# The FFNs' activated tiles in four groups, read by the second matrix's products four columns from each group in turn

## The chip, the core and the metric

The kernel runs on one core of a Trainium2 chip. The metric is the device time of one execution in microseconds (us); 2208.91 us is the median of three runs before the change. The engines are named as the profile names them: PE is TensorE (the products), PEld its weight loads, DVE VectorE, ACT ScalarE, POOL GpSimd, SP SyncE.

## What is computed

One inference step of a decoder layer over 256 prompt tokens and 32 sample tokens, 288 tokens in all, with a model width of 2048: a gated FFN, a recurrent mixer, and a second gated FFN, each between two RMSNorms. The change is in the two FFNs alone:

```
D_MODEL = 2048
D_FF = 5632

def swiglu(x, w_in, w_out):
    gate, up = jnp.split(x @ w_in, 2, axis=-1)
    return (jax.nn.silu(gate) * up) @ w_out

x = x + 0.5 * rmsnorm(swiglu(rmsnorm(x, g[0]), ffn1_w_in[l], ffn1_w_out[l]), g[1])
...
x = x + 0.5 * rmsnorm(swiglu(rmsnorm(x, g[4]), ffn2_w_in[l], ffn2_w_out[l]), g[5])
```

## The kernel before

Activations stand with the channels on the 128 partitions and the 288 tokens along the free axis: one tile of 128 x 288 for each 128 channels. A product takes 128 x 128 weights as the stationary operand, streams 288 columns of activations, and adds 128 x 288 sums into a PSUM tile.

Everything is split into a high and a low part, both of type float32r, so one float32 product is three products: high weights by high activations (L596), high weights by low activations (L597), low weights by high activations (L598). The function `mm3` yields these three. The weights come by DMA on SP's queue as `raw` tiles of 128 x 1024 (512 KB); ACT copies the high part into a `wh` tile (L100), DVE subtracts to get the low part (L101). Three `raw` and four `wh` buffers are in turn, so that the splitting runs ahead of the products.

The function `block` makes one group of output columns: 512 wide, so four PSUM tiles (f = 0 to 3), over `nk` tiles of the contraction (k). A `wh` unit holds two k. For each unit the order is f, then k, then the three products, 24 products a unit. The order on every engine is the order in which the code is written, with some instructions moved behind a named one.

The FFN function `ffn` cuts the 5632 hidden channels into 11 chunks of 512. For chunk c, `do_in` makes a `gate` and an `up` block (nk = 16, from the tiles `xh`, `xl`). `ev_up` takes a finished `up` tile: DVE multiplies it by the norm's row (L691) and by the gate (L692), ACT writes the high part into `hh` (L693), DVE the low part into `hl` (L694). `do_out` then makes four `out` blocks (o = 0 to 3) from `hh` and `hl` with 4 k for each chunk and adds the result to `y` (L782). The chunks are staggered: in 0, in 1, out 0, in 2, out 1, up to in 10, and last one out stage over the chunks 9 and 10 together (nk = 8). So each FFN has 10 out stages: nine that an in stage follows, and the last one.

Before the change `hh` and `hl` are tiles of 128 x 4 x 288: for each of the chunk's four k the 288 tokens lie one behind the other, 1152 bytes. A column of the products' moving operand is one token.

Of the kernel before, what the change touches and what calls it, by code (L numbers as in the profile page):

```python
# [9 lines left out]
F32 = mybir.dt.float32  # L10
F32R = mybir.dt.float32r
U8 = mybir.dt.uint8
AF = mybir.ActivationFunctionType
# [18 lines left out]
RAW_BUFS = 3  # L32
HL_BUFS = 4
HALF = 1024 + 32
SCAN_LAG = 4
X_EARLY = 12

# [93 lines left out]
def trunk_kernel(ctx, tc, x_prompt, x_sample, state_gla, state_hgrn, norm_gains, f1_in, f1_out, f2_in, f2_out,  # L131
# [455 lines left out]
    def block(name, nk, rhs, evac, width=512, tick=None, tail=1, hold=False, most=99, fill=None, late=0, byk=(), lag=0, skip=()):  # L587

        nf, per = width // P, 1024 // width
        nu = nk // per  # L590
        ps = [mmtile(f"{name}_{f}") for f in range(nf)]
        ws = [W.next() for _ in range(EARLY // per)] if fill else []

        def mm3(dst, w, f, k, parts, start, stop):
            a, c = k % per, slice(f * P, f * P + P)
            yield lambda: PE.matmul(dst, w[0][:, a, c], parts[0], start=start, stop=False)  # L596
            yield lambda: PE.matmul(dst, w[0][:, a, c], parts[1], start=False, stop=False)  # L597
            yield lambda: PE.matmul(dst, w[1][:, a, c], parts[0], start=False, stop=stop)  # L598

        def mm(w, f, k):  # L600
            if not fill or f or k >= EARLY:
                for ready in mm3(ps[f][:, 0:T], w, f, k, rhs(k), k == 0, k == nk - 1):
                    product[0] = ready().ins

        if fill:
            fill.products(lambda dst, k, parts, stop: mm3(dst, ws[k // per], 0, k, parts, k == 0, stop), ps[0][:, 0:T])
        for u in range(nu - tail):
            w = ws.pop(0) if ws else W.next()
            if u not in byk:
                for f in range(nf):  # L610
                    for k in range(u * per, (u + 1) * per):
                        mm(w, f, k)
                    if tick is not None and f % 2:
                        tick(u * per + f // 2)
            for k in range(u * per, (u + 1) * per) if u in byk else ():
                if fill and k < UPDATED:

                    fs = range(1 if k < EARLY else 0, nf)
                    threes = [list(mm3(ps[f][:, 0:T], w, f, k, rhs(k), k == 0, False)) for f in fs]
                    for three in threes:  # L620
                        three[0]()
                        product[0] = three[2]().ins
                    with tc.issue_after(product[0]):
                        for three in threes:
                            product[0] = three[1]().ins
                elif k < late:

                    threes = [list(mm3(ps[f][:, 0:T], w, f, k, rhs(k), k == 0, False)) for f in range(nf)]
                    for ready in [r for t in threes for r in t[:2]] + [t[2] for t in threes]:
                        product[0] = ready().ins  # L630
                else:
                    for f in range(nf):
                        mm(w, f, k)
                if tick is not None:
                    tick(k)
            if u not in skip and not (lag and u == nu - tail - 1):
                W.ahead(most)
            if fill and u == 5:
                fill.scaled()
        ws = [W.next() for _ in range(tail)]  # L640
        ks = range((nu - tail) * per, nk)
        ticked = 0
        for f in range(nf):
            for k in ks:
                mm(ws[k // per - (nu - tail)], f, k)
            ins = evac(f, fill.total(ps[f][:, 0:T]) if fill and f == 0 else ps[f][:, 0:T])
            while tick is not None and (ticked + 1) * nf <= (f + 1) * len(ks):
                tick(ks[ticked])
                ticked += 1
            if lag and f == lag:  # L650
                with tc.issue_after(ins):
                    W.ahead(most)
        if not hold:
            W.ahead()
# [4 lines left out]
    def ffn(tag, gcol, gnext, pn, before, fill=None):  # L659
# [3 lines left out]
        with ExitStack() as pools:  # L663
# [1 line left out]
            hid, final_tiles = {}, []  # L665

            def do_in(c):
                hh = fp.tile([P, 4, T], F32R, name=f"hh{tag}_{c}", tag="hh")
                hl = fp.tile([P, 4, T], F32R, name=f"hl{tag}_{c}", tag="hl")
                hid[c] = (hh, hl)  # L670
                gs = []

                def gate(g):
                    def run():
                        V.tensor_tensor(g, g, rt, op=ALU.mult)
                        act(g, g, AF.Silu)
                    return run

                def ev_gate(f, ps):
                    g = fp.tile([P, T], F32, name="g", tag="g", bufs=6)  # L680
                    gs.append(g)
                    if c == 0:
                        W.behind = S.activation(g, ps, AF.Copy).ins
                        pn.late.append(gate(g))
                    else:
                        V.tensor_tensor(g, ps, rt, op=ALU.mult)
                        act(g, g, AF.Silu)

                def ev_up(f, ps):
                    u = fp.tile([P, T], F32, name="u", tag="u", bufs=3)  # L690
                    ins = V.tensor_tensor(u, ps, rt, op=ALU.mult).ins  # L691
                    V.tensor_tensor(u, u, gs[f], op=ALU.mult)  # L692
                    S.activation(hh[:, f, :], u, AF.Copy)  # L693
                    V.tensor_tensor(hl[:, f, :], u, hh[:, f, :].bitcast(F32), op=ALU.subtract)  # L694
                    return ins

                if c == 0:
                    block(f"gate{tag}_0", KT, xrhs, ev_gate, tick=pn.tick0, most=1 if final else 0, fill=fill,
                          late=0 if final else FIRST, byk=range(KT))
                    before.close()  # L700
                    if not final:
                        border.append(Border(mixer_start, hg1, gnext, 5, 2))
                else:
                    block(f"gate{tag}_{c}", KT, xrhs, ev_gate, byk=(2,) if c == 1 else ())
                if final and c == 0:
                    last_pool()
                block(f"up{tag}_{c}", KT, xrhs, ev_up, tick=pn.tick1 if c == 0 else None,
                      byk=(0,) if c == 1 or final and c == 0 else (), lag=int(c == 0))

# [49 lines left out]
            def do_out(c, n):  # L759
# [8 lines left out]
                for o in range(4):  # L768
                    def ev(f, ps):
# [17 lines left out]
                        if end:  # L787
                            if not final:
                                border[0].fill.new(k)
                            elif k < KT - 1:  # L790
# [6 lines left out]
                                else:  # L797
                                    if f > 1:
                                        by_token(zs[f - 2], k - 2, *zt)
                                    zs.append(z)  # L800
                    block(f"out{tag}_{c}_{o}", 4 * n, lambda k: [t[:, k % 4, :] for t in hs[k // 4]], ev,
                          tail=2 if end and o == 3 else 1, hold=end and o == 3)
                    k = 4 * (c - 4) + o
                    if final and 0 <= k < KT:
# [928 lines left out]
```

## Time and profile before

| | us |
|---|---|
| runs | 2209.27, 2208.91, 2207.38 |
| median | 2208.91 |
| span of the profiled execution | 2206.5 |

The profile is of one execution of its own; its span runs from the first to the last instruction, and what lies around it isn't listed apart: the runs are 0.9 to 2.8 us longer than the span.

| engine | busy us | share of the span |
|---|---|---|
| PE | 2198.2 | 100% |
| PEld | 2182.2 | 99% |
| DVE | 1385.7 | 63% |
| ACT | 1020.1 | 46% |
| POOL | 180.0 | 8% |

A busy PE does not mean a PE at its peak: a product's record includes its way through the array, so records overlap, and what counts is the distance from one start to the next. In the rows of groups, a line, an engine and an operation are followed by the tile written and the tiles read, the shape and the count; behind the bar stand the busy time in us, the mean of one in ns, the engine's idle time just before them in us and what ended it. In the view by stretches each row has the stretch in us from the span's start, its length, the busy time of each engine with the number of instructions that touch the stretch, the granted clock, the DMA engines' share and GB/s.

### The profile page before, as it was taken

Reading aid. Unit: us, or ns where it says so; the run is one execution under the profiler, and the core shown is the slowest. Engines: PE = TensorE matmul, PEld = TensorE weight load, DVE = VectorE, ACT = ScalarE, POOL = GpSimd, SP = SyncE. Lnnn points to the kernel's source line nnn. Section 1 sums busy time; section 2 is a strip of 40 time slices with the busy share of each in tenths; the row PEclk is TensorE's granted clock in tenths of the full one; section 3 lists DMA queues with packets and bytes.
Section 4 is the critical chain, followed back from the end, with each engine's and each line's share of the span. In section 5 each row is a group of like instructions: output and inputs, shape, how many; then the busy total and the mean of one; then the engine's idle time right before and its main releaser. Section 6 shows DMA issues by size and latency. Waiting matters only on the chain.

```text
span 2206.5 us, 43225 instructions
## 1 busy us (share of the span) xinstructions
PE 2198.2 (100%) x17828; PEld 2182.2 (99%) x17828; DVE 1385.7 (63%) x2253; ACT 1020.1 (46%) x1537; POOL 180.0 (8%) x327
## 2 busy tenths in 40 slices
PE   9999999999999999999999999999999999999998
PEld 9999999999999999999999999999999999999998
DVE  7545546555555568888888755844555466556646
ACT  6443433343344345655676654543333333333344
POOL 2000000000000001233210000000000020122005
PEclk9999999999999999999999999999999999999999
DMA  7655555555555554667566564555555565666555
GB/s 223 174 166 171 169 168 170 171 165 171 172 166 180 179 166 142 194 207 216 173 189 176 176 190 135 169 167 171 171 166 170 172 176 172 180 179 179 172 164 161
DMA packets 227334, 384.87 MB, mean 174 GB/s; under 512 B 21362, under 2 KB 60864, under 8 KB 227136
## 3 DMA queue, kind: packets, MB, share of 16 engines
q1 hardware_dynamic: 213872, 365.02, 55.1%
q0 software_dynamic: 10992, 16.77, 2.8%
q8 instruction: 140, 2.29, 0.4%
q10 hardware_dynamic: 2272, 0.31, 0.1%
q14 instruction: 58, 0.48, 0.1%
HBM read 363.75 MB, written 11.80 MB: 170 GB/s over the span
## 4 chain that ended last, share of the span: by engine, by line
PE 98%; DVE 1%; ACT 1%; issue 0%; POOL 0%; DVEq 0%; ACTq 0%; POOLq 0%
PE gate L597 10%; PE gate L596 10%; PE gate L598 10%; PE up L597 8%; PE out L597 8%; PE up L596 8%; PE up L598 8%; PE out L596 8%; PE out L598 8%; PE hfq L596 2%; PE hfq L597 2%; PE mo L597 2%; PE hfq L598 2%; PE mo L596 1%; PE mo L598 1%; PE hi L597 1%
## 5 line engine op out<-in xcount | busy, mean ns | idle before, releaser
L101 DVE TENSOR_TENSOR wh<-raw,wh 128x1024 fp32r<-128x1024 f32 (+1 forms) x676 | 821.7, 1217 | 610.2 <-ACT wh L100 609.1
L100 ACT ACTIVATE wh<-raw 128x1024 fp32r<-128x1024 f32 (+1 forms) x676 | 711.0, 1053 | 943.1 <-PE gate L598 295.2
L597 PE MATMUL gate<-xl,wh 128*128 128x288 f32 x1660 | 490.1, 297 | 0.0
L598 PE MATMUL gate<-xh,wh 128*128 128x288 f32 x1660 | 483.6, 293 | 0.0
L596 PE MATMUL gate<-xh,wh 128*128 128x288 f32 x1660 | 483.0, 292 | 0.0
L597 PE MATMUL out<-hl,wh 128*128 128x288 f32 x1408 | 419.2, 298 | 0.0
L597 PE MATMUL up<-xl,wh 128*128 128x288 f32 x1408 | 419.2, 298 | 0.0
L598 PE MATMUL up<-xh,wh 128*128 128x288 f32 x1408 | 411.6, 292 | 0.0
L598 PE MATMUL out<-hh,wh 128*128 128x288 f32 x1408 | 411.5, 292 | 0.0
L596 PE MATMUL out<-hh,wh 128*128 128x288 f32 x1408 | 409.3, 291 | 0.0
L596 PE MATMUL up<-xh,wh 128*128 128x288 f32 x1408 | 409.3, 291 | 0.0
L596 PEld LDWEIGHTS gate<-xh,wh 128*128 128x128 f32 x1660 | 313.7, 189 | 0.8 <-DVE u L691 0.4
L598 PEld LDWEIGHTS gate<-xh,wh 128*128 128x128 f32 x1660 | 311.4, 188 | 0.2 <-DVE wh L101 0.2
L597 PEld LDWEIGHTS gate<-xl,wh 128*128 128x128 f32 x1660 | 310.2, 188 | 0.5
L596 PEld LDWEIGHTS out<-hh,wh 128*128 128x128 f32 x1408 | 266.8, 189 | 0.2 <-DVE y L782 0.2
L596 PEld LDWEIGHTS up<-xh,wh 128*128 128x128 f32 x1408 | 266.7, 189 | 0.0
L598 PEld LDWEIGHTS up<-xh,wh 128*128 128x128 f32 x1408 | 264.5, 188 | 0.0
L598 PEld LDWEIGHTS out<-hh,wh 128*128 128x128 f32 x1408 | 264.5, 188 | 0.0
L597 PEld LDWEIGHTS up<-xl,wh 128*128 128x128 f32 x1408 | 263.8, 187 | 0.0
L597 PEld LDWEIGHTS out<-hl,wh 128*128 128x128 f32 x1408 | 263.7, 187 | 0.0
L782 DVE TENSOR_TENSOR y<-out,y 128x288 f32<-128x288 f32 x287 | 120.7, 452 | 82.1 <-PE out L598 81.1
L739 POOL DMA_DIRECT2D xT<-b x64 | 37.1, 586 | 757.3 <-PE gate L598 566.7
(417 smaller groups left out, 2559.1 us busy)
## 6 DMA issues: line engine op xcount, KB each, us to landing
raw<-in_ffn_w_in_dram SPq DMA_DIRECT2D x350, 512.0 KB, 3.6
raw<-in_ffn_w_out_dram SPq DMA_DIRECT2D x176, 512.0 KB, 3.6
raw<-in_mix_w_in_dram SPq DMA_DIRECT2D x64, 512.0 KB, 4.3
raw<-in_mix_w_in_dram SPq DMA_DIRECT2D x96, 256.0 KB, 3.2
raw<-in_mix_w_out_dram SPq DMA_DIRECT2D x32, 512.0 KB, 3.7
out_dram<-s POOLq DMA_DIRECT2D x32, 256.0 KB, 2.9
s<-in_state_gla_dram SPq DMA_DIRECT2D x16, 256.0 KB, 5.9
s<-in_state_hgrn_dram SPq DMA_DIRECT2D x16, 256.0 KB, 5.6
```

The source lines that it names most:

```text
L100: i1 = self.nc.scalar.activation(h[:, a, c], raw[:, a, c], AF.Copy).ins
L101: i2 = self.nc.vector.tensor_tensor(l[:, a, c], raw[:, a, c], h[:, a, c].bitcast(F32), op=ALU.subtract).ins
L596: yield lambda: PE.matmul(dst, w[0][:, a, c], parts[0], start=start, stop=False)
L597: yield lambda: PE.matmul(dst, w[0][:, a, c], parts[1], start=False, stop=False)
L598: yield lambda: PE.matmul(dst, w[1][:, a, c], parts[0], start=False, stop=stop)
L739: queues[n % len(queues)].dma_start(dst[q * TS:(q + 1) * TS, 4 * g:4 * g + 4, :, cols].rearrange("p k t c -> p (k t) c"), b32[rows, q])
L782: V.tensor_tensor(y[k], ps, y[k], op=ALU.add)
```

## The change

Each `hh` and `hl` tile becomes 128 x 4 x 4 x 80. The 288 tokens of one k are cut into four groups of 72, and a group has 80 places, so that the groups begin 320 bytes apart and eight places of each stay unused. A k takes 1280 bytes instead of 1152, and each of the four buffers grows by 512 bytes a partition. ACT and DVE write the groups through the same pattern (4 x 72).

The products of the out blocks read these tiles in turns: four columns from group 0, four from group 1, four from group 2, four from group 3, then the next four of each, 18 turns. The PSUM tile is addressed in the same way, its 288 columns as four groups of 72 without gaps, so each token's sum lands at the column where it landed before, and what reads the PSUM tile is unchanged. `mm3` takes this path where the activations have three dimensions, which only the FFNs' `out` blocks give it.

```diff
+LINE = 4
+PLACES = 4
+
+def columns(t):
+    return t.rearrange("p (g c) -> p g c", g=PLACES)
+
+def turns_of(t):
+    return t.rearrange("p g (i e) -> p i g e", e=LINE)
...
         def mm3(dst, w, f, k, parts, start, stop):
             a, c = k % per, slice(f * P, f * P + P)
+            if len(parts[0].shape) == 3:
+                dst, parts = turns_of(columns(dst)), [turns_of(t) for t in parts]
             yield lambda: PE.matmul(dst, w[0][:, a, c], parts[0], start=start, stop=False)
...
-                hh = fp.tile([P, 4, T], F32R, name=f"hh{tag}_{c}", tag="hh")
-                hl = fp.tile([P, 4, T], F32R, name=f"hl{tag}_{c}", tag="hl")
+                hid[c] = [fp.tile([P, 4, PLACES, 80], F32R, name=f"h{j}{tag}_{c}", tag=f"h{j}") for j in "hl"]
+                hh, hl = ([t[:, f, :, 0:T // PLACES] for f in range(4)] for t in hid[c])
                 hid[c] = (hh, hl)
...
-                    S.activation(hh[:, f, :], u, AF.Copy)
-                    V.tensor_tensor(hl[:, f, :], u, hh[:, f, :].bitcast(F32), op=ALU.subtract)
+                    S.activation(hh[f], columns(u), AF.Copy)
+                    V.tensor_tensor(hl[f], columns(u), hh[f].bitcast(F32), op=ALU.subtract)
...
-                    block(f"out{tag}_{c}_{o}", 4 * n, lambda k: [t[:, k % 4, :] for t in hs[k // 4]], ev,
+                    block(f"out{tag}_{c}_{o}", 4 * n, lambda k: [t[k % 4] for t in hs[k // 4]], ev,
```

No instruction changes its place on any engine; lines move down by 15. On PE, at the start of the first out block (`out_0_0_0` is chunk 0, o = 0, f = 0; `hh_0`, `hl_0` are chunk 0's tiles), there stands before:

```order
L596 MATMUL out_0_0_0_1463<-hh_0_235,wh_1351 128x288
L597 MATMUL out_0_0_0_1463<-hl_0_236,wh_1351 128x288
L598 MATMUL out_0_0_0_1463<-hh_0_235,wh_1351 128x288
L596 MATMUL out_0_0_0_1463<-hh_0_235,wh_1351 128x288
L597 MATMUL out_0_0_0_1463<-hl_0_236,wh_1351 128x288
L598 MATMUL out_0_0_0_1463<-hh_0_235,wh_1351 128x288
```

and after the change, at the same place:

```order
L611 MATMUL out_0_0_0_1463<-hh_0_235,wh_1351 128x18x4x4
L612 MATMUL out_0_0_0_1463<-hl_0_236,wh_1351 128x18x4x4
L613 MATMUL out_0_0_0_1463<-hh_0_235,wh_1351 128x18x4x4
L611 MATMUL out_0_0_0_1463<-hh_0_235,wh_1351 128x18x4x4
L612 MATMUL out_0_0_0_1463<-hl_0_236,wh_1351 128x18x4x4
L613 MATMUL out_0_0_0_1463<-hh_0_235,wh_1351 128x18x4x4
```

Only the shape is new: 18 turns, four groups, four columns.

## The prediction

> **What bounds the kernel now.** I read the page first: engines, the clock, the chain, then the groups of the products that the change touches.
>
> ```profile
> span 2206.5 us, 43225 instructions
> PE 2198.2 (100%) x17828; PEld 2182.2 (99%) x17828; DVE 1385.7 (63%) x2253; ACT 1020.1 (46%) x1537; POOL 180.0 (8%) x327
> PEclk9999999999999999999999999999999999999999
> PE 98%; DVE 1%; ACT 1%; issue 0%; POOL 0%; DVEq 0%; ACTq 0%; POOLq 0%
> L597 PE MATMUL out<-hl,wh 128*128 128x288 f32 x1408 | 419.2, 298 | 0.0
> L598 PE MATMUL out<-hh,wh 128*128 128x288 f32 x1408 | 411.5, 292 | 0.0
> L596 PE MATMUL out<-hh,wh 128*128 128x288 f32 x1408 | 409.3, 291 | 0.0
> ```
>
> TensorE is 98% of the chain, at the full granted clock, and idles 0.0 us before the out products. So the time is the number of products times the step from one to the next. The 291 to 298 ns of a product are no step: products overlap. The step comes from the time order of TensorE (start, duration, line, tile), and from the view by stretches for the whole last out stretch:
>
> ```profile
> 198.83 0.29 PE L596 MATMUL out<-hh,wh 128*128 128x288 f32 x1
> ...
> 205.07 0.29 PE L596 MATMUL out<-hh,wh 128*128 128x288 f32 x1
> ...
> 2143.48:2180.92 37.44, 37.44 (x290) 1.00 0.60 179
> ```
>
> The two starts enclose one out block of 4 x 4 x 3 = 48 products by the code: 6.24 us / 48 = 130.0 ns. The last FFN's three blocks of 96 give 37.44 / 288 = 130.0 ns again (the x290 counts products that only reach in). The step is the same at both ends of the run, so something regular sets it. The weight loads show its inside (PEld is TensorE's weight load; each row starts as the product before it starts to stream):
>
> ```profile
> 198.71 0.19 PEld L596 LDWEIGHTS out<-hh,wh 128*128 128x128 f32 x1
> 198.84 0.19 PEld L597 LDWEIGHTS out<-hl,wh 128*128 128x128 f32 x1
> 198.96 0.19 PEld L598 LDWEIGHTS out<-hh,wh 128*128 128x128 f32 x1
> 199.10 0.19 PEld L596 LDWEIGHTS out<-hh,wh 128*128 128x128 f32 x1
> 199.23 0.19 PEld L597 LDWEIGHTS out<-hl,wh 128*128 128x128 f32 x1
> ```
>
> Steps of 0.13, 0.12, 0.14, 0.13: equal columns, unequal steps. The step during which L598's weights are loaded is the long one, as L597's mean of 298 ns against L596's 291 says too. Another stretch of the same shape has yet another step:
>
> ```profile
> 988.37 0.29 PE L596 MATMUL hi<-xh,wh 128*128 128x288 f32 x1
> ...
> 995.91 0.29 PE L596 MATMUL hi<-xh,wh 128*128 128x288 f32 x1
> ...
> 988.37:995.91 7.54, 7.54 (x59) 1.00 0.28 75
> ```
>
> Here 57 products take 7.54 us, 132.3 ns each, with only 75 GB/s of DMA against 179 above. Same columns, same clock, same three lines; the step depends on how the streams stand to each other. As each product streams while the next weights are read, I take these two reads to be what meets.
>
> **The rule against it.** The Trainium skill, SBUF — State Buffer, section "Who interferes with whom", gives TensorE two independent read ports and says that "PE and ACT never wait on anyone"; by that the reading order could change nothing. The rows of 130.0 and 132.3 ns don't fit a stream that nothing delays, though they don't prove that the load delays it. Its weight is the second case below.
>
> **The change, part by part.** *Out products.* There are 2 FFNs x 11 chunks x 16 column tiles x 4 x 3 = 4224 (the three group rows: 3 x 1408). They are 4224 x 130.0 ns = 549.1 us of the span. Their number, order and loads stay; each moving read becomes 72 runs of four columns (16 bytes), one from each group in turn, the groups 320 = 256 + 64 bytes apart. A contiguous read stays 16 columns in each 64 bytes, the weights' read too. If the two disturb each other by nearness in such a place, the changed read is there for four columns in sixteen instead of a long stretch, so a collision is short and can be made good. The trace has no such read. Bounds for the step: above, no gain, 130.0 ns; below, the shortest step in the rows, 0.12, which rounding leaves between 0.115 and 0.125. I take 0.125, its cautious end, since the rows near it are 0.13: 4224 x 5.0 ns = **21.1 us less**. At 122.5 ns it would be 31.7 us less; if only L597 and L598 came down to L596's duration, (7 + 1) / 3 = 2.7 ns a step, 11.3 us less.
>
> The Trainium skill, TensorE: Matmul & The Clock Gate, section "Back-to-back issue gap", gives N / 2.4 + 2.5 ns for a warm product: an estimate of 122.5 ns for 288 columns, by which 31.7 us would go.
>
> *Lost step after a switch.* 18 times an out block hands over to an in block (9 per FFN). The 7.54 us above show that a stretch may run 57 products at 132.3 before it settles: 57 x 2.3 = 0.13 us, 18 times 2.4 us. From below nothing, as every switch now happens at an even pace; from above an in chunk that never settles, 18 x 384 x 2.3 ns = 15.9 us. I take **2.0 us more**, near the stretch that was seen.
>
> *Writing the activated tiles.* 88 activations and 88 subtractions now write 4 x 72.
>
> ```profile
> L693 ACT ACTIVATE hh<-u 128x288 fp32r<-128x288 f32 x88 | 37.4, 445 | 58.1 <-DVE u L692 57.8
> L262 ACT ACTIVATE xh<-x,prm 128x288 fp32r<-128x288 f32 x36 | 18.0, 531 | 18.7 <-DVE x L568 16.9 <-DVE x L350 1.8
> L694 DVE TENSOR_TENSOR hl<-u,hh 128x288 fp32r<-128x288 f32 x88 | 37.9, 451 | 0.1
> L100 ACT ACTIVATE wh<-raw 128x1024 fp32r<-128x1024 f32 x670 | 708.4, 1059 | 943.1 <-PE gate L598 295.2 <-PE up L598 243.4 <-PE out L598 145.3
> L694 DVE TENSOR_TENSOR hl<-u,hh x88: 447/451/459, 63.1 to 2147.7; 128x288 fp32r<-128x288 f32 x88
> ```
>
> From below nothing; from above the slowest ACT row of 288 elements, 531 ns, 88 x 86 = 7.6 us of ACT. ACT sits 943 us idle before its weight splits, waiting for TensorE to free a buffer. That covers it: **0**. Only the last chunk is used at once: its last subtraction ends at 2147.7 + 0.45 = 2148.2, and the block that began at 2143.48 reaches that chunk's first columns 48 products later, at 2149.7. The 1.5 us left hold 16 such additions; without that cover each would delay the end by itself.
>
> *Supply.* At 125 ns a unit of 24 products lasts 3.00 us instead of 3.12, so 512 KB must come in 3.00 us: 175 GB/s.
>
> ```profile
> GB/s 223 174 166 171 169 168 170 171 165 171 172 166 180 179 166 142 194 207 216 173 189 176 176 190 135 169 167 171 171 166 170 172 176 172 180 179 179 172 164 161
> ```
>
> Slices of 194 to 223 GB/s stand there, and a split costs ACT 1.06 us a unit: **0**; uncovered, the step would stay at 130.
>
> *Writing PSUM.* The result is written in the same order: runs of 16 bytes, 288 bytes apart. The nearest rows are small products, L1128 writing two runs of 16 columns, L1120 one run of 32:
>
> ```profile
> L1120 PE MATMUL sc<-rp,one 128*32 128x32 f32 x96 | 2.2, 201 | 0.0
> L1128 PE MATMUL sc<-R,k_h 128*32 128x32 f32 x16 | 1.4, 196 | 0.0
> ```
>
> One break costs nothing there (196 against 201). From above, one column's time per break: 130.0 / 288 = 0.45 ns x 72 = 32.5 ns a product. I take **0**, near the rows, and keep the rest as a rival. The Trainium skill, Advanced Engine Details and Errata, section "PSUM Cachelines", says that any non-contiguous pattern "significantly slows down matmuls", and in its next line that two consecutive elements should lie together for best throughput; four do here, so the two lines point apart and the trace has no row to judge between them.
>
> **Sum.** -21.1 + 2.0 = -19.1 us. The span would be 2206.5 - 19.1 = 2187.4; the runs lie 0.9 to 2.8 us over the span, their median 2.4, so 2208.9 - 19.1 = **2189.8**, say 2190.
>
> **The rivals.** *No change.* The step is set by something that keeps its pace whatever the order, the products' own reading rate or the weight load. For it:
>
> ```profile
> 1054.59 0.40 PE L1385 MATMUL sn<-bd,ks 96*128 96x512 f32 x1
> 1054.82 0.29 PE L596 MATMUL hfq<-xh,wh 128*128 128x288 f32 x1
> ```
>
> 512 columns took 0.23 us to the next start, 0.45 ns a column, as much as 130.0 / 288 = 0.45, though only one weight load stood beside them, as beside 288. A fixed number of collisions per load would be diluted there. Against it: 130.0 and 132.3 for one shape. It gives 2209, with the switches up to 2211.
>
> *Slower by the breaks in PSUM.* Each break in the written pattern holds the array. It decides from 5.0 / 72 = 0.07 ns a break on, where it eats the gain. At a column's time, 32.5 ns x 4224 = 137 us: 2346; at every second break 2277. For it speaks only that the trace has no product with so many breaks; against it L1128.
>
> *Slower by the read itself.* The weights' place is now under some line of every turn, so no stretch is free of collisions and the out blocks run at the unsettled 132.3: 4224 x 2.3 = 9.7 us more, 2219. It decides where the step exceeds 130.0. That the step of before is so even (130.0 at both ends) says that contiguous streams can find a good phase; broken ones need not.
>
> *The change doesn't do what it says:* excluded, since all 4224 products show the new shape in the order of instructions, and only those.
>
> **How the numbers follow.** Forecast with its partial forms (2175 to 2204): 0.55. No change: 0.18. Slower by the read: 0.12. Slower by PSUM: 0.15. Likeliest is 2190. The range runs from 122.5 ns without loss at the switches, 2177 less the 2 us by which the runs differ, 2175, to 2222, which takes in no change and the unsettled step (2219 with the same 2 to 3 us); it leaves out PSUM's case and a little below. About 0.2%, 4.4 us, can be told from no change: faster 0.55, same 0.18, slower 0.27.
>
> **What would show it.** Right: an out block of 48 products in 6.00 us, L597's mean near L596's, in blocks still at 130.0 after a few triples, TensorE still idle 0.0 us. No change: 6.24 us with the new shape. PSUM: all three lines longer by tens of ns alike. The read: 6.35 us and uneven. Wrong altogether if TensorE begins to wait for hh, hl or wh, or if the in blocks lose their 130.0.

## The result and the profile after

| | runs | median us | lowest to highest |
|---|---|---|---|
| before | 9 | 2207.84 | 2207.12 to 2209.27 |
| after | 9 | 2202.28 | 2201.16 to 2203.17 |

After by before is 0.9973, with a 95% interval of 0.9964 to 0.9982: the change is faster by 5.6 us, where 19 were forecast. The profiled executions say the same: a span of 2201.3 us, before 2206.5.

The page after, with the rows that answer to those of before (engines, chain, the three groups of out products):

```profile
span 2201.3 us, 43226 instructions
PE 2192.4 (100%) x17828; PEld 2175.8 (99%) x17828; DVE 1385.3 (63%) x2253; ACT 1020.0 (46%) x1537; POOL 180.0 (8%) x327
PE 97%; DVE 1%; ACT 1%; DMA 1%; issue 0%; POOL 0%; ACTq 0%; DVEq 0%; POOLq 0%
L611 PE MATMUL out<-hh,wh 128*128 128x288 f32 x1408 | 408.9, 290 | 0.0
L613 PE MATMUL out<-hh,wh 128*128 128x288 f32 x1408 | 408.7, 290 | 0.0
L612 PE MATMUL out<-hl,wh 128*128 128x288 f32 x1408 | 408.0, 290 | 0.0
```

TensorE bounds as before and idles 0.0 us before the out products. The three lines, 291, 298 and 292 ns before, are even now: 290 each. That is what the forecast wanted to see; the step is not. TensorE's rows in order of time, the first three of an out block and the first of the next:

```profile
185.53 0.29 PE L611 MATMUL out<-hh,wh 128*128 128x288 f32 x1
185.66 0.29 PE L612 MATMUL out<-hl,wh 128*128 128x288 f32 x1
185.79 0.29 PE L613 MATMUL out<-hh,wh 128*128 128x288 f32 x1
...
191.69 0.29 PE L611 MATMUL out<-hh,wh 128*128 128x288 f32 x1
```

48 products take 6.16 us, 128.3 ns each. The view by stretches for one out stage (192 products), the in chunk behind it (384 products) and the last stage's three blocks (288 products):

```profile
185.53:210.17 24.64, 24.64 (x194) 1.00 0.55 171
210.17:260.12 49.95, 49.95 (x386) 1.00 0.57 169
2138.43:2175.39 36.96, 36.96 (x290) 1.00 0.63 181
```

24.64 / 192 = 128.33 ns, and 36.96 / 288 = 128.33 again, at the full clock. The same out stage and in chunk before:

```profile
186.35:211.31 24.96, 24.96 (x194) 1.00 0.56 169
211.31:261.23 49.92, 49.92 (x386) 1.00 0.56 169
```

So 4224 products save 1.67 ns each, 7.0 us, and each in chunk behind an out stage pays 0.03 us, 18 times 0.5 us. One thing stands in the profiled execution beside that. In the mixer's last blocks, which the change doesn't touch, ACT waits for a weight transfer, its PSUM reads come late, and TensorE waits for them 0.30 us and then once more, 0.36 us (order of time, after: ACT's split and TensorE's weight load, in brackets the idle time ahead and what ended it):

```profile
1284.81 1.06 ACT L113 ACTIVATE wh<-raw 128x1024 fp32r<-128x1024 f32 x1 [1.19 <-DMA raw<-in_mix_w_out_dram]
...
1286.22 0.19 PEld L611 LDWEIGHTS mo<-xh,wh 128*128 128x128 f32 x1 [0.30 <-ACT y L1681]
```

From there three blocks of 192 products take 76.96 us. The stretches of all three, of the second of them, and of out stage 8, after:

```profile
1285.20:1362.16 76.96, 76.75 (x579) 1.00 0.58 175
1311.32:1336.71 25.39, 25.39 (x195) 1.00 0.54 166
707.64:732.28 24.64, 24.64 (x195) 1.00 0.64 191
```

The same three blocks and out stage 8 before:

```profile
1289.59:1364.56 74.97, 74.97 (x579) 1.00 0.58 176
710.51:735.79 25.28, 25.27 (x195) 1.00 0.60 189
```

The second of the three blocks has no wait left and still steps at 25.39 / 192 = 132.2 ns, where all three step at 130.0 or close to it before (74.97 / 576 = 130.2). The kernels of the experiments below have the same blocks, and their traces say more. The wait is not the change's: the run of "Places, contiguous", without turns, has one of 0.38 us there, and 132.2 ns behind it. Nor does it always move the step: the run of "The weights' place" and the better version with 112 bytes have 0.36 and 0.35 us and keep 130.0. No run without such a wait has 132.2 there.

From the first product behind the first FFN's last out stage to the first out product of the second FFN, the profiled execution is 1.7 us longer in all (635.65 us, before 633.95). The sum is -7.0 + 0.5 + 1.7 = -4.8 us, and -5.1 with the 0.3 of a disturbed block of before (25.28 us in out stage 8, where its others take 24.96), against -5.2 in the spans. Across nine runs the medians differ by 5.6, so the mixer's part need not be in every run.

### The profile page after: what moved, and what is told of

Same layout as the page of the kernel before. It is cut to its first block, busy times and chain, and to the rows that moved or that the text cites. A ratio compares the mean times of both kernels' runs of the same rounds, so it can differ in the third digit from the quotient of the medians.

```text
span 2201.3 us, 43226 instructions
## 1 busy us (share of the span) xinstructions
PE 2192.4 (100%) x17828; PEld 2175.8 (99%) x17828; DVE 1385.3 (63%) x2253; ACT 1020.0 (46%) x1537; POOL 180.0 (8%) x327
## 4 chain that ended last, share of the span: by engine, by line
PE 97%; DVE 1%; ACT 1%; DMA 1%; issue 0%; POOL 0%; ACTq 0%; DVEq 0%; POOLq 0%
PE gate L612 10%; PE gate L611 10%; PE gate L613 10%; PE up L612 9%; PE up L611 8%; PE up L613 8%; PE out L613 8%; PE out L611 8%; PE out L612 8%; PE hfq L611 2%; PE hfq L612 2%; PE hfq L613 2%; PE mo L613 1%; PE mo L612 1%; PE mo L611 1%; PE hi L612 1%
## 5 line engine op out<-in xcount | busy, mean ns | idle before, releaser
L612 PE MATMUL out<-hl,wh 128*128 128x288 f32 x1408 | 408.0, 290 | 0.0
```

## The experiments

In all of them "step" is the time from the first product of a chunk's out stage to the first one behind it, by the number of products (192 in four blocks). Each chunk of each FFN can have a form of its own, so one run holds some twenty measurements. Each run was profiled once; a form that stands in several runs has the same step in each to 0.1 ns (the change's 128.3 in seven, 127.3 with 112 bytes in three), so tenths of a ns can be read. The theory at the start was the forecast's: the moving read meets the load of the next weights, and what is lost is lost there. Its rivals were that the product's own read sets the step, or the pattern written to PSUM.

**Fewer columns.** The out products read and write the first n of the 288 tokens, contiguous as before the change. `form` is a table by FFN and chunk: groups, their distance, the run, the shift in the buffer, the columns, and whether reading and writing go in turns. The next two runs use the same code with other tables.

```diff
+def moving(t, tag, c):
+    g, pitch, line, off, n, src, dst = form(tag, c)
+    v = view(t, tag, c)
+    if src:
+        return turns(v, line)
+    return v if g > 1 else v[:, 0, 0:n]
...
+            if name.startswith("out"):
+                tag, chunk = name[3:].split("_")[0:2]
+                dst, parts = target(dst, tag, int(chunk) + k // 4), [moving(t, tag, int(chunk) + k // 4) for t in parts]
```

> The layout of before (one run of 288 tokens), but each chunk's out products stream only the first n columns of the 288: 288, 256, 224, 192, 160, 128, 96, 64, 32 for chunks 0 to 8 of the first FFN, 288, 272, 240, 208, 176, 144, 112, 80, 48 in the second; the other tokens' sums of those chunks are left out. The two reads collide (mine): a collision costs the streaming product, so the step falls with the columns and keeps an excess of some 5 to 8 ns, 256 at about 116 and 224 at about 103. The reading keeps its own rate: 0.45 ns a column, 256 at 115.6, 192 at 86.7, until the weight load is the longer one. The weight load sets the step: 130 at 256 and 224 as at 288, and no fall at all until the load has no company.

Measured: 130.0 ns at 288 columns, 124.4 at 272, 117.8 at 256, 112.9 at 224 and about 112 from there down to 112 columns. The stretches of 288, 256 and 160 columns:

```profile
111.17:136.13 24.96, 24.96 (x195) 1.00 0.57 170
186.05:208.66 22.61, 22.61 (x195) 1.00 0.60 186
401.81:423.39 21.58, 21.58 (x194) 1.00 0.63 189
```

Below some 240 columns something else sets about 112 ns, a number that does not change with the columns; the weight load is there for every product and is the natural candidate, though no run shows it: in the run with narrower weights below, a load's record grows from 94 ns for 16 columns to 187 for 128, 0.83 ns a column, so an estimate for 128 columns is 106 ns. At 288 that floor is 18 ns away: the load's length alone does not set the step. The whole run took 2246.9 us, longer with less work, because in the stages of 96 columns and fewer the granted clock fell to 0.50 and the step rose to 213 ns.

**Places, contiguous.** The contiguous read is moved in its buffer, some bytes further by chunk.

```diff
-                hh = fp.tile([P, 4, T], F32R, name=f"hh{tag}_{c}", tag="hh")
+                hh = fp.tile([P, 4, WIDE[int(tag) - 1]], F32R, name=f"hh{tag}_{c}", tag="hh")
...
+def view(t, tag, c):
+    g, pitch, line, off, n, src, dst = form(tag, c)
+    return groups(t[:, off:off + g * pitch], g)[:, :, 0:T // g]
```

> One run of 288 tokens as before, only shifted within a wider tile by chunk: first FFN (1408 bytes a k, the same 128 over a multiple of 256 as before) 0, 16, 32, 64, 128, 192, 224, 240, 256 bytes, second FFN (1280 bytes a k, a multiple of 256) 0 to 128 bytes in steps of 16. The two reads collide by place: the step of an out block changes with the shift by some ns, and at 256 bytes it is that of 0 again; the second FFN differs from the first, since k moves only the weights there. The reading's own rate, or the load: 130.0 at every shift.

With 1408 bytes a k: 130.0 at 0 and at 256 bytes, 131.2 at 32, 132.2 at 16, 64, 224 and 240, 132.9 at 192, 133.3 at 128. With 1280 bytes a k 131.2 to 133.3, nowhere 130.0. The stretches at 0, 128 and 256 bytes:

```profile
111.47:136.43 24.96, 24.96 (x194) 1.00 0.58 170
412.13:437.73 25.60, 25.60 (x195) 1.00 0.54 165
715.43:740.39 24.96, 24.96 (x194) 1.00 0.62 185
```

The same columns in the same order, and 3.3 ns between two places. The place counts, 0 and 256 bytes agree, and the kernel before stood at the best of these.

**Turns.** Reads in turns of other kinds, and reading and writing changed apart.

```diff
+def target(t, tag, c):
+    g, pitch, line, off, n, src, dst = form(tag, c)
+    if dst:
+        return turns(groups(t, dst), line)
+    return t[:, 0:n]
```

> Forms of the turns by chunk. First FFN, read and written in turns: four groups 288, 320, 352, 384, 416, 448 and 512 bytes apart with runs of 4, then 320 bytes with runs of 8 and of 24. Collisions by place: 320 and 448 (64 bytes more or less than a multiple of 256) at 128.3, 512 (all four in one place) at 130 or more, 384 between, longer runs back towards 130. Second FFN: chunk 0, turns read at 320 bytes but PSUM written in one run (its sums then stand in another token order); chunk 1, one run read and PSUM written in turns; 2 and 3 two groups 640 and 576 bytes apart; 4 four groups of 320 bytes read one after the other; 5 runs of 2; 6 eight groups of 160; 7 three of 384; 8 six of 192. If the breaks in PSUM take part of the gain back: chunk 0 at about 125, chunk 1 at 133. If they cost nothing: chunk 0 at 128.3 and chunk 1 at 130.0, all else by the read alone.

| read | step, ns |
|---|---|
| four groups 320 bytes apart, runs of 4, PSUM written in turns (the change) | 128.33 |
| the same read, PSUM written straight | 128.33 |
| contiguous read with 1280 bytes a k, PSUM written in turns | 132.21 |
| contiguous read with 1280 bytes a k, PSUM written straight (the run of "Places, contiguous") | 132.21 |
| the change's tiles read one group after the other, no turns, PSUM written straight | 132.2 |
| four groups 288, 352, 384, 416, 448 bytes apart | 132.2, 132.2, 135.6, 131.1, 130.6 |
| four groups 512 bytes apart | 151.9 |
| runs of 8, of 24 columns, 320 bytes apart | 131.1, 134.5 |
| two groups, 640 and 576 bytes apart | 137.8, 136.7 |
| three groups 384, six 192, eight 160 bytes apart | 136.9, 131.2, 133.4 |
| runs of two columns, 320 bytes apart | 252.1 |

The stretches with 512 bytes, with the change's read and PSUM written straight, with the contiguous read and PSUM in turns, and with the change's tiles read without turns:

```profile
562.97:592.14 29.17, 29.17 (x195) 1.00 0.47 145
1477.42:1502.06 24.64, 24.64 (x195) 1.00 0.59 171
1552.00:1577.39 25.39, 25.39 (x195) 1.00 0.56 167
1779.90:1805.28 25.38, 25.38 (x194) 1.00 0.55 167
```

PSUM's breaks cost nothing, from either side. The reading order alone makes the difference, and of many orders the change's is the fastest here. The last row of the view takes the change apart: its tiles read without turns step at 132.2 ns, 2.2 more than before the change, and the turns on the same tiles bring 3.9. What was measured as 1.67 is the difference of the two. Runs of two take 252.1 / 144 = 1.75 ns a run, and the change's runs of four 128.33 / 72 = 1.78: a run of two costs as much as one of four. That would be a price of about 1.75 ns for each read of up to four columns, and 126 ns for 72 of them.

**Places, in turns.** The change's read, moved by 0 to 240 bytes.

```diff
+                hid[c] = [fp.tile([P, SIZE[int(tag) - 1]], F32R, name=f"h{j}{tag}_{c}", tag=f"h{j}") for j in "hl"]
+                hh, hl = hid[c] = [[view(t, f, tag, c) for f in range(4)] for t in hid[c]]
...
+    step, pitch, off = form(tag, c)
+    return t[:, f * step + off:f * step + off + 3 * pitch + 72] if pitch == 72 else \
+        t[:, f * step + off:f * step + off + 4 * pitch].rearrange("p (g c) -> p g c", g=4)[:, :, 0:72]
```

> The changed kernel's turns (four groups 320 bytes apart, runs of four), each chunk's tiles shifted within a wider tile. First FFN: 1408 bytes a k (128 over a multiple of 256, so that k moves activations and weights alike), shifts of 0, 16, 32 up to 144 bytes by chunk. Second FFN: 1280 bytes a k as in the change, shifts of 32, 64, 96, 128, 160, 192, 224, 16, 48 and 0 bytes. If the step is set by where a run meets the weights' place, the turns too have good and bad shifts, 2 to 5 ns apart, with a best of 125 to 128; shifts by 64 bytes, which only change the place a turn begins with, count less than those by 16 and 32. If turns spread every collision evenly, 128.3 at every shift.

> The rest of the same sweep. First FFN: 1408 bytes a k with shifts of 160 to 240 bytes; 1344 bytes a k with 0 and 64; 1472 with 0 and 64. Second FFN: 1280 bytes a k with 80, 112, 144, 176, 208, 240 bytes; then one run of 288 tokens without turns at 1152, 1280 and 1216 bytes a k; last chunks as in the change. Place decides: good and bad shifts as in the other half; without turns 130.0 at 1152 and 132.2 at 1280 as measured before. Turns spread collisions evenly: 128.3 at every shift of the turns.

With the change's 1280 bytes a k (FFN2): 128.3 at 0, 127.8 at 16, 129.1 at 32, 128.6 at 48, 127.5 at 64, 129.2 at 80, 129.7 at 96, 127.3 at 112, 128.4 at 128, and much the same 128 bytes further on (127.5 at 192, 129.7 at 224, 127.2 at 240). With 1408 bytes a k 127.8 to 132.2, with 1344 129.1 at both places tried; one stage with 1472 had a disturbed block and 130.1 behind it. Without turns 1152 bytes a k gave 130.0 and 1280 132.2, as measured before, and 1216 132.4. No place gave less than 127.2: turns don't make the product indifferent to its place, and don't bring it to 125.

**Narrower weights.** If the load is what the read meets, less to load must help.

```diff
+                part, narrow = dst[0:n], slice(f * P, f * P + n)
+                yield lambda: PE.matmul(dst if start else part, w[0][:, a, c if start else narrow], parts[0], start=start, stop=False)
+                yield lambda: PE.matmul(part, w[0][:, a, narrow], parts[1], start=False, stop=False)
+                yield lambda: PE.matmul(dst if stop else part, w[1][:, a, c if stop else narrow], parts[0], start=False, stop=stop)
```

> The out products load narrower weights: by chunk 0 to 7 of each FFN 128, 112, 96, 80, 64, 48, 32 and 16 columns instead of 128 (in 10 of the 12 products of a chain; the first and the last keep 128), chunks 8 to 10 keep 128; the sums of the other output channels lack those products. The moving read stays whole: in FFN1 as before the change (contiguous, 1152 bytes a k), in FFN2 as after it (turns of four columns, groups 320 bytes apart). Theory: what a product loses above its 288 columns at full rate is lost where the load's read and the moving read meet. The run with fewer columns gave 0.42 ns a column and an excess of some 10 ns a product, so with half of the weights' columns to read about half of it goes: 130.0 at 128, about 125 at 64 and 121 to 122 at 16 columns in FFN1; 128.3, 124 and 121 in FFN2. Rival: the excess belongs to the product itself (its own reading, or a fixed gap between products): 130.0 and 128.3 at every width. Rival 2: it depends on the place alone and not on how much is loaded, so that the step jumps between 127 and 132 without a trend.

The loads did get shorter, as the groups of weight loads with 128, 64 and 16 columns show:

```profile
L644 PEld LDWEIGHTS out<-hl,wh 128*128 128x128 f32 x512 | 96.0, 187 | 0.0
...
L644 PEld LDWEIGHTS out<-hl,wh 128*64 128x64 f32 x128 | 17.2, 134 | 0.0
L644 PEld LDWEIGHTS out<-hl,wh 128*16 128x16 f32 x128 | 12.0, 94 | 3.4
```

The step did not. The stretches with 128 and 16 columns of weights, contiguous (first two) and in turns (last two):

```profile
111.34:136.30 24.96, 24.96 (x194) 1.00 0.57 170
638.04:663.32 25.28, 25.28 (x195) 1.00 0.55 168
1471.60:1496.24 24.64, 24.64 (x194) 1.00 0.57 171
1994.44:2018.91 24.47, 24.47 (x194) 1.00 0.56 173
```

Contiguous 130.0, then 132.2, 132.2, 132.6, 132.2, 131.6, 131.8 and 131.6 with 112 down to 16 columns; in turns 128.3, then 127.2, 128.1, 127.9, 127.8, 127.5, 126.7 and 127.5. In turns an eighth of the load takes 0.9 ns away, where 7 were expected, and no width takes more than 1.6; in the contiguous form the eighth adds 1.6. The theory of the start has fallen: how much is loaded isn't what a product pays for.

**Two k in a stretch.** A form of the change without unused bytes.

```diff
+def paired(t, k, s):
+    b = k // 2 * 576 + k % 2 * 72 + s
+    return t[:, b:b + 576].rearrange("p (g c) -> p g c", g=4)[:, :, 0:72]
```

> The change without its unused bytes: two k share a stretch of 2304 bytes, four groups 576 bytes apart (64 above a multiple of 256, as 320 is), the even k in the first half of each group and the odd k 288 bytes behind it (32 above a multiple of 256); the products still read four columns from each group in turn. In FFN1 the tiles start 0, 16, 32, up to 112 bytes further on (chunks 0 to 7, hh and hl alike; chunk 8: 160, last 112); in FFN2 hh starts at 112 bytes and hl at 0, 16 up to 96 and at 128 (chunks 0 to 7; chunk 8: hh 0, hl 112; last both 112). Theory of the place (only where a run of four stands modulo 128 bytes decides, for each k by itself): each step is the mean of the two places' steps in the runs with shifts, so 127.4 to 127.6 at 112 bytes (127.3 and 127.7), about 128.6 at 64 bytes, 129 to 130 at 32 bytes. Rival: the step is set by how the whole sequence of products falls into a rhythm, so that two places in turn give other steps than their mean, up to 131 to 132 in places. If the 112 bytes give 127.5, this form needs no more memory than before and can be had for all activations.

FFN1: 127.0 at 0, 129.8, 127.8, 128.6, 129.0, 129.7, 128.5 and 128.7 at 16 to 112 bytes; FFN2 (hh and hl apart) 127.9 to 131.0. 112 bytes gave 128.7 where the mean of the places said 127.4 to 127.6, and 0 bytes 127.0 where the same mean (128.3 at 0, 129.1 at 32) is 128.7. A step is not the mean of what its places give by themselves, and the best place has to be tried.

**More columns.** Does a product lose a fixed time, or does it read slowly throughout?

```diff
+                n, b = READ[min(c2, 9)], k % 4 // 2 * 576
+                dst = ps[f][:, 0:n]
+                if tag == "1":
+                    parts = [t[:, b:b + n] for t in parts]
+                else:
+                    parts = [turns(four(t[:, b + s:b + s + 576])[:, :, 0:n // 4]) for t in parts]
```

> After the run with narrower weights, which left the step where it was, the load is no partner: what a product loses, it loses in its own read. Here the out products read more columns than there are tokens: by chunk 304, 288, 320, 352, 384, 416, 448, 480, 512 and 288 (an odd k reads with the even one's activations, columns behind the 288th are not used, and in FFN2 the tokens' sums stand in another order). FFN1 reads contiguous stretches; FFN2 reads four columns in turn from four groups 576 bytes apart, starting at 112 bytes, and writes PSUM straight. Theory of a gap for each product: 288 columns at full rate are 120.0 ns, and 8 to 10 ns come on top once a product, so 384 columns take 169 ns and 512 take 222 in both forms, and the turned form keeps its 1.5 to 3 ns less at every length. Theory of a slower rate (each read of four columns takes 1.78 to 1.81 ns in place of 1.67): contiguous 384 columns 173.3 and 512 columns 231 ns; turned 170 to 171 and 227 to 228, so that the gain of the turns grows with the columns, to 3 to 5 ns.

The stretches of 288, 384 and 512 columns, contiguous (three rows) and in turns (three rows):

```profile
187.72:213.10 25.38, 25.38 (x194) 1.00 0.56 166
422.54:455.82 33.28, 33.28 (x195) 1.00 0.44 128
773.54:818.13 44.59, 44.59 (x194) 1.00 0.39 117
1629.48:1653.92 24.44, 24.44 (x194) 1.00 0.57 173
1862.16:1895.32 33.16, 33.16 (x194) 1.00 0.45 129
2211.19:2255.34 44.15, 44.15 (x194) 1.00 0.35 107
```

Contiguous 132.2, 173.3 and 232.2 ns, in turns 127.3, 172.7 and 230.0: 0.442 to 0.459 ns a column, where the theory of a fixed gap had 222 at 512 columns. From 288 to 512 columns the contiguous step grows by 100.0 ns, 0.446 a column, which leaves less than 4 of the 132.2 ns for anything fixed; in turns it grows by 102.7, and nothing is left. The read is slow throughout, the theory of the gap has fallen. But the gain of the turns doesn't grow either: 4.9 ns at 288, 2.2 at 512, and at 352 the turns are slower (161.1 against 160.0).

**Bad orders with narrow weights.** Are the bad orders bad by themselves?

```diff
+                n = LOADED[int(tag) - 1][min(int(chunk) + k // 4, 9)]
+                part, narrow = dst[0:n], slice(f * P, f * P + n)
```

> The worst orders of reading, with weights of 128 columns and of fewer (in 10 of the 12 products of a chain, so that the sums of the other output channels lack them). FFN1 by chunk: turns of four from four groups 512 bytes apart with 128, 64, 32 and 16 columns of weights; contiguous with 16; groups 384 bytes apart with 128 and 16; turns of 24 columns, groups 320 bytes apart, with 128 and 16; last contiguous with 128. FFN2: two groups 640 bytes apart with 128 and 16; runs of two columns with 128 and 16; three groups 384 bytes apart with 128 and 16; the change's form with 128 and 16, then 128. Theory of the own read: the step stays as wide weights gave it: 151.9 at 512 bytes for every width, 135.6 at 384, 134.5 with turns of 24, 137.8 with two groups, 252 with runs of two, 136.9 with three groups, 128.3 and about 127.5 for the change's form. Theory of the meeting: with 16 columns there is next to nothing to meet, and all but the runs of two come down to the same 127 to 130.

The stretches of groups 512 bytes apart and of two groups, each with 128 and with 16 columns of weights:

```profile
111.61:140.78 29.17, 29.17 (x195) 1.00 0.48 146
348.69:377.72 29.03, 29.03 (x194) 1.00 0.47 145
1490.83:1517.28 26.45, 26.45 (x194) 1.00 0.54 160
1567.21:1593.51 26.30, 26.30 (x195) 1.00 0.53 161
```

151.9 and 151.2; 137.8 and 136.9; runs of two 252.1 and 249.0; 384 bytes apart 135.6 and 133.4, as three groups 136.9 and 132.5; runs of 24 134.5 and 133.3; the change's own form 128.3 and 127.5. What a bad order costs stays for the most part with next to no load to meet, least of all with three groups, where 5.0 of 8.6 ns over the change's form are left. So most of it lies in the read's own sequence. That runs hinder each other when they come from the same place would fit the groups 512 bytes apart, which are all in one place modulo 256; it is not shown, and two groups 576 bytes apart, 64 over a multiple of 256, are slow too (136.7). The load's part is 0.7 to 4.5 ns.

**The weights' place.** Moving and weights moved apart and together.

```diff
-        h, l = hl[:, :, 0:512], hl[:, :, 512:1024]
+        h, l = hl[:, :, s:s + 512], hl[:, :, s + 512:s + 1024]
```

> The split weights of the out blocks stand some bytes further on in their buffers, by chunk, and so does the moving operand. FFN1 reads contiguous as before the change; (moving, weights) in bytes by chunk 0 to 9: (0,0), (0,64), (0,128), (64,64), (64,0), (128,128), (128,0), (0,32), (32,32), (0,0). FFN2 reads in turns as the change does: (0,0), (112,0), (0,16), (0,64), (0,128), (112,112), (112,64), (112,16), (96,0), (112,0). Theory of the own read (a product loses time to its own read alone, the load has no part): the weights' place changes nothing; 130.0 wherever moving is 0 in FFN1, 132.2 at 64, 133.3 at 128, 131.2 at 32; in FFN2 128.3 at 0, 127.3 at 112, 129.7 at 96. Theory of the meeting (where the two reads stand to each other decides; with fewer weights only the start of the load is left, so it would have to be the start that counts): equal shifts give the step of no shift, 130.0 at (64,64), (128,128) and (32,32), and 128.3 at (112,112); unequal ones go as the moving operand's shift did: about 132.9 at (0,64), 133.3 at (0,128), 132.2 at (0,32); in FFN2 127.3 at (0,16), 127.5 at (0,64), 129.7 at (112,16).

The contiguous stretches of (0,0), (0,64), (0,128), (64,64) and (128,128) bytes:

```profile
111.57:136.53 24.96, 24.96 (x194) 1.00 0.56 170
186.46:211.98 25.52, 25.52 (x195) 1.00 0.53 165
261.92:287.52 25.60, 25.60 (x195) 1.00 0.54 165
338.29:363.68 25.39, 25.39 (x195) 1.00 0.55 166
488.94:513.92 24.98, 24.98 (x194) 1.00 0.56 170
```

130.0, 132.9, 133.3, 132.2 and 130.1. Moving the weights alone by 128 bytes costs what moving the read alone did, and moving both takes it back; (0,32) gave 132.3, and (32,32) 130.0 in its last two blocks, after a disturbed one. (64,64) should have given 130.0 and did not. In turns (0,64) gave 127.5 as foreseen, but (0,16) 128.5 for 127.3, (112,16) 128.2 for 129.7 and (112,112) 129.0 for 128.3. So neither pure theory stands: the load has a part in the step by where it stands, up to 3.3 ns here, and neither place alone nor their distance foretells it.

**Better versions, timed.** First the change with hh and hl 112 bytes further on; then the same with all other activations in turns too, two k in a tile.

```diff
+                hid[c] = [fp.tile([P, 1344], F32R, name=f"h{j}{tag}_{c}", tag=f"h{j}")[:, 28:1308] for j in "hl"]
+                hh, hl = ([columns(t[:, f * 320:f * 320 + 320])[:, :, 0:T // PLACES] for f in range(4)] for t in hid[c])
```

> The change with one thing more: each hh and hl tile begins 112 bytes further on in its buffer (176 above a multiple of 256, in place of 64). In the run with shifts these groups gave 127.3 ns in FFN2 against 128.3 of the change. Theory of the place (where the runs of four stand decides the step, and nothing else that differs between the FFNs): 127.3 ns in both FFNs, 4224 x 1.0 ns = 4.4 us less than the change, 11.6 us less than before: 2196 to 2198. Rival: the sequence falls into another rhythm and steps of 128.3 to 130 come back in part: 2199 to 2203.

2197.70 us (2196.76 to 2198.47, 5 runs), ratio to before 0.9952 (0.9940 to 0.9965). The step is 127.3 in all out stages, 4224 x 2.7 = 11.4 us less by the rows, 10.5 by the medians.

```diff
+    pairs = [[xpool.tile([P, PLACES, T // 2], F32R, name=f"x{j}{k}") for k in range(KT // 2)] for j in "hl"]
+    xh, xl = [[p[k // 2][:, :, k % 2 * 72:k % 2 * 72 + 72] for k in range(KT)] for p in pairs]
...
+                S.activation(xh[t], columns(y[t]), AF.Copy)
+                V.tensor_tensor(xl[t], columns(y[t]), xh[t].bitcast(F32), op=ALU.subtract)
```

> As the one with hh and hl 112 bytes further on, and the activations of all other blocks (xh, xl: FFN in blocks, the mixer's blocks and its last ones, 11928 products) stand in turns too: two k share a tile of 2304 bytes in four groups 576 bytes apart, the odd k 288 bytes behind the even one, no bytes more than before; the products read four columns from each group in turn. In the run with pairs this form gave 127.0 ns at this place (FFN1, chunk 0) and 127.8 to 130 at others. If it keeps 127.0 in the in blocks and the mixer, 11928 x 3.0 = 36 us less, 2162 in all; at 128.3 20 us less, 2178. If the gain belongs to the out blocks alone (their order of reading, hh and hl of one chunk beside each other), the in blocks stay at 130.0 or go to 132: 2196 or 2220. The writing of xh and xl in groups costs ACT and DVE nothing that shows, as with hh and hl.

2164.68 us (2164.42 to 2166.97, 5 runs), ratio to before 0.9803 (0.9790 to 0.9816): 43.5 us, nearly eight times what the change brought. An out stage and the in chunk behind it in this kernel:

```profile
183.38:207.84 24.46, 24.46 (x194) 1.00 0.56 172
207.84:256.56 48.72, 48.72 (x386) 1.00 0.58 173
```

48.72 / 384 = 126.9 ns in the in blocks (130.0 before), 127.4 in the out blocks. The gain does not belong to the out blocks; they were only the smaller part of the products.

## Why the prediction missed the size

*What bounds.* Right. TensorE is 97% of the chain, idles 0.0 us before the out products, and its step is what changed.

*Out products, -21.1 us.* This is the term that failed: **the step is 128.33 ns and not 125, the term -7.0 us.** The forecast took the shortest step in the rows, 0.12, as one that every product could have once collisions with the weight load were short. Four things speak against that reading. The difference of two starts that are each rounded to 0.01 us can be off by 0.01, so 0.12 allowed 0.11 to 0.13, not 0.115 to 0.125; the trace has 198.836 and 198.964 there, 128 ns. The products' own starts in before come in triples of 126, 133 and 131 ns, and only the mean of 130 is a step that all can have; single steps of 125 stand in the out blocks after as well, whose mean is 128.33. With an eighth of the load the step stays within 1.6 ns, so collisions with the load did not fill the 5 ns that the forecast wanted to save. And the read takes 0.442 to 0.459 ns a column up to 512 columns, so it is slow throughout; 72 reads at the 1.75 ns that a run of two shows are 126 ns, and no block of 48 products of 288 columns came out below 126.6 ns in any run with full loads.

A second thing was left out of the sum: the tiles' new distances, 320 bytes between groups and 1280 between k, were priced at nothing. Read without turns they give 132.2 ns, so the turns' 3.9 ns went in good part to make up for them. What could be had was 130.0 less some 126.7, and of these 3.3 ns the change got 1.67; 112 bytes further on give 2.7.

That the reading order alone changes the step was right, and so was the sign for these distances. That it does so by nearness to the load was half right at most: the weights' place counts for up to 3.3 ns, their amount for little (2.6 ns at the most in these two forms, and not always less with fewer columns), and what makes bad orders bad is for the most part the read's own sequence.

*The rule on two ports* (the Trainium skill, SBUF — State Buffer, "Who interferes with whom") gives the moving read and the load ports that don't hinder each other. For the amount loaded the runs nearly agree (131.6 with 16 columns, 130.0 with 128). For the place they don't: 133.3 against 130.0 with nothing moved but the weights. *The rule on the gap* (TensorE: Matmul & The Clock Gate of the Trainium skill, "Back-to-back issue gap") gives an estimate of 122.5 ns at 288 columns and 215.8 at 512; measured were 126.6 at the least and 230.0 to 232.2. The section states it for an isolated product and not for a stream with a weight load each, which this kernel is. The lower end of the forecast's range, 122.5 ns, has no other source; no run shows it.

*Lost step after a switch, +2.0 us.* Too high: 0.03 us a switch, 0.5 in all. The in chunk has its 130.0 almost at once.

*Writing the activated tiles and supply, 0.* Right, as the groups of ACT show: the writing takes 445 ns as before, and ACT still sits 939 us idle before its splits (943 before).

```profile
L113 ACT ACTIVATE wh<-raw 128x1024 fp32r<-128x1024 f32 x670 | 708.4, 1059 | 939.2 <-PE gate L613 295.6 <-PE up L613 245.4 <-PE out L613 147.1
L708 ACT ACTIVATE hh<-u 128x288 fp32r<-128x288 f32 x88 | 37.5, 445 | 58.1 <-DVE u L707 57.8
```

*Writing PSUM, 0.* Right: 128.33 with and without the breaks. But the rows beside it didn't say so. In the kernel it is L1120 that writes two runs of 16 columns and L1128 that writes one of 32, the other way round, so they read 201 ns with a break and 196 without; and they are durations, not steps. That 0 came out was luck. Of the two lines that the prediction quoted from the Trainium skill (Advanced Engine Details and Errata, "PSUM Cachelines"), the first doesn't hold for runs of 16 bytes.

*The rivals.* "No change" had named the reading's own rate, and its row of 512 columns at 0.45 ns a column was the better witness: the rate is real, but it depends on the order. The prediction itself added that "a fixed number of collisions per load would be diluted there"; that sentence was right and should have weighed more. "Slower by the read" fell for this layout alone: groups 288, 352 or 384 bytes apart come out at 132 to 136 ns, and no other distance of that run came below 130.0. So 320 was a fortunate choice, and even the sign was in part luck.

*What stays open.* Whether a read of four columns really has a price of about 1.75 ns and what makes it, why a whole sequence settles at one even step rather than another, and why (64,64) bytes do not bring back 130.0. The runs show that these things happen, not what in the memory makes them.

## What to carry to other kernels

Where one engine is the whole chain, a step that is shorter in some rows is not yet a step that all can have: take the mean over a whole block, not the difference of two rounded starts, and look for a longer instruction of the same kind that tells a rate from a fixed loss. Where a change alters the layout and the order of reading, time the new layout in the old order too: here one lost 2.2 ns and the other won 3.9. The layout of a moving operand, its groups and its place modulo 128 or 256 bytes, is worth one run with a form for each chunk, since neighbouring places differ by up to 3% and can't be summed from their parts. And a gain of 1 to 3 ns a product is to be sought for all products at once: on a quarter of them it was 5.6 us, with a better place and on all of them 43.5.

## What was not expected of the hardware

- Runs of two float32 columns take 252.1 ns where runs of four take 128.3, and four groups in one place modulo 256 bytes 151.9, with the load at an eighth of its columns as well (249.0, 127.5 and 151.2).
- The same contiguous products of the mixer run at 130.0 ns in most runs and at 132.2 in two. Both times a wait of 0.30 to 0.38 us stood before, and the step stayed changed for more than 400 products; in two other runs such a wait changed nothing.
- In every stage of products of 96 columns and fewer the granted clock fell to 0.50; at 112 columns it stayed at 1.00. TensorE in a stage of 64 columns:

```profile
655.00:670.00 15.00, 15.00 (x72) 0.50 0.32 88
```

  15 us hold 72 products that touch it, some 213 ns each, about twice the 110 ns that the first block of 96 columns took at the full clock.
